# RMSNorm with doubled rows on one core: loads moved between the two DMA queues, the last tile loaded whole, and 60 drains at the head of two engines' programs

## Chip, cores and metric

The kernel runs on one core of a Trainium2 chip. The time is device time in microseconds (us). The kernel before took 240.69 to 241.01 us in four runs.

## The reference

```python
B, S, D = 8, 512, 2048
x_rep  = np.repeat(x, 2, axis=1)                       # every row twice
rms    = np.sqrt((x_rep ** 2).mean(axis=-1, keepdims=True) + 1e-6)
return ((x_rep / rms) * gamma[None, None, :]).astype(np.float32)
```

The input has 33.6 MB, the output 67.1 MB, all float32. Arithmetic is light (VectorE is busy 38% of the span and ScalarE 48%, the DMA engines 98.3%), so the work is mostly moving bytes.

## The kernel before

There are eight tiles of 128 partitions x 4 rows. A tile's buffer holds 8 rows: the input lands in rows 4 to 7, the results go to rows 0 to 7, and there are three buffers. ScalarE squares and sums a row and takes the root. VectorE inverts it and scales the row. The second copy of each row is made by ScalarE (three of four) or VectorE. Loads are issued on ScalarE's DMA queue, stores on SyncE's. The load of tile i+1 waits until the store of tile i-2 has left its buffer.

```python
    def load(i, eng, parts=1):
        y = rows.tile([P, K * R, D], f32, name="y")
        step = K // parts
        for k in range(0, K, step):
            at = K * (R - 1) + k
            eng.dma_start(out=y[:, at : at + step, :], in_=x_t[i, :, k : k + step, :])
        ys.append(y)

    def store(i, k0, k1):
        run = 32768 if i == ntiles - 3 else 65536
        nc.sync.dma_start(
            out=out_t[i, :, R * k0 * D : R * k1 * D],
            in_=ys[i][:, R * k0 : R * k1, :].rearrange("p j d -> p (j d)"),
            max_dma_last_dim=run,
        )
    # ... (square, scale, repeat, compute left out)
    load(0, nc.scalar, parts=K)
    gamma_b = singles.tile([P, D], f32, name="gamma_b")
    nc.sync.dma_start(out=gamma_b[0:1, :], in_=gamma.partition_broadcast(1))
    # ... (gamma's broadcast and eps left out)
    load(1, nc.scalar)
    load(2, nc.scalar)
    for i in range(ntiles):
        if i >= 2 and i + 1 < ntiles:
            load(i + 1, nc.scalar, parts=2 if i + 2 == ntiles else 1)
        parts = 2 if i == ntiles - 1 else 1
        for k in range(0, K, K // parts):
            compute(i, k, k + K // parts)
            store(i, k, k + K // parts)
```

Of the kernel before, what the change touches and what calls it, by code (L numbers as in the profile page):

```python
# [1 line left out]

# [4 lines left out]


@with_exitstack
def kernel(  # L10
    ctx: ExitStack,
    tc: tile.TileContext,
    x: bass.AP,
    gamma: bass.AP,
    out: bass.AP,
):
    nc = tc.nc
    P = nc.NUM_PARTITIONS
    f32 = mybir.dt.float32
    Act = mybir.ActivationFunctionType  # L20
    Alu = mybir.AluOpType

    B, S, D = x.shape
    Bo, So, Do = out.shape
    R = So // S
    assert R == 2 and D == Do and B == Bo and So == S * R
    eps = 1e-6
    inv_d = 1.0 / float(D)


    K = 4
    N = B * S
    assert N % (P * K) == 0
    ntiles = N // (P * K)
    x_t = x.rearrange("b s d -> (b s) d").rearrange("(n p k) d -> n p k d", p=P, k=K)
    out_t = out.rearrange("b s d -> (b s) d").rearrange("(n p j) d -> n p (j d)", p=P, j=K * R)

    singles = ctx.enter_context(tc.tile_pool(name="singles", bufs=1))
    rows = ctx.enter_context(tc.tile_pool(name="rows", bufs=3))
    junk = ctx.enter_context(tc.tile_pool(name="junk", bufs=1, space=bass.MemoryType.PSUM))  # L40
    small = ctx.enter_context(tc.tile_pool(name="small", bufs=8))

    ys = []
# [9 lines that stand above are left out]
        ys.append(y)  # L53

    def store(i, k0, k1):

        run = 32768 if i == ntiles - 3 else 65536
        nc.sync.dma_start(  # L58
            out=out_t[i, :, R * k0 * D : R * k1 * D],
            in_=ys[i][:, R * k0 : R * k1, :].rearrange("p j d -> p (j d)"),  # L60
            max_dma_last_dim=run,
        )

    def square(i, k):
        sq = junk.tile([P, D], f32, name="sq")
        ss = small.tile([P, 1], f32, name="ss")
        nc.scalar.activation(  # L67
            out=sq[:], in_=ys[i][:, K * (R - 1) + k, :], func=Act.Square, accum_out=ss[:]
        )
        rms = small.tile([P, 1], f32, name="rms")  # L70
        nc.scalar.activation(out=rms[:], in_=ss[:], func=Act.Sqrt, scale=inv_d, bias=eps_t[:])  # L71
        return rms

    def scale(i, k, rms):
        rstd = small.tile([P, 1], f32, name="rstd")
        nc.vector.reciprocal(out=rstd[:], in_=rms[:])  # L76
        nc.vector.scalar_tensor_tensor(  # L77
            out=ys[i][:, R * k, :], in0=ys[i][:, K * (R - 1) + k, :], scalar=rstd[:], in1=gamma_b[:],
            op0=Alu.mult, op1=Alu.mult,
        )  # L80

    def repeat(i, k, copy):
        copy(out=ys[i][:, R * k + 1, :], in_=ys[i][:, R * k, :])  # L83

    def compute(i, k0, k1):

        rms = square(i, k0)
        for k in range(k0, k1):
            scale(i, k, rms)
            if k + 1 < k1:  # L90
                rms = square(i, k + 1)
                repeat(i, k, nc.scalar.copy)
            else:
                repeat(i, k, nc.vector.tensor_copy)


    ctx.enter_context(tc.manual_schedule())
    load(0, nc.scalar, parts=K)
    gamma_b = singles.tile([P, D], f32, name="gamma_b")
    nc.sync.dma_start(out=gamma_b[0:1, :], in_=gamma.partition_broadcast(1))  # L100
    nc.gpsimd.partition_broadcast(out_ap=gamma_b[:], in_ap=gamma_b[0:1, :])  # L101
    eps_t = singles.tile([P, 1], f32, name="eps_t")
    nc.vector.memset(eps_t, eps)  # L103
    load(1, nc.scalar)
    load(2, nc.scalar)

    for i in range(ntiles):


        if i >= 2 and i + 1 < ntiles:  # L110
            load(i + 1, nc.scalar, parts=2 if i + 2 == ntiles else 1)
        parts = 2 if i == ntiles - 1 else 1
        for k in range(0, K, K // parts):
            compute(i, k, k + K // parts)
            store(i, k, k + K // parts)


# [1 line left out]
_INS = ['x', 'gamma']  # L119
_OUTS = [((8, 1024, 2048), 'float32')]  # L120


# [23 lines left out]
```

## Time and profile before

| | before |
|---|---|
| time, median of 3 runs | 240.72 us |
| span of the profiled run | 239.0 us |
| 16 DMA engines, two data queues | 98.3% of the span |
| ScalarE / VectorE busy | 48% / 38% |
| two 8 KB instruction packets at | 87.0 and 148.8 us |

The page of the kernel before, its first three parts. In part 2 a digit is the busy share of a fortieth of the span in tenths. In part 3 a line is a DMA queue (q1 is SyncE's, q10 ScalarE's, q14 the one that the page calls instruction) with packets, megabytes and its share of the 16 engines' time.

```profile
span 239.0 us, 295 instructions
...
DVE 90.8 (38%) x74; ACT 115.8 (48%) x121; POOL 2.5 (1%) x5
...
DMA  7999989989979989999899899799999999898994
...
q1 hardware_dynamic: 1426, 67.12, 65.0%
q10 hardware_dynamic: 1728, 33.56, 33.3%
q14 instruction: 2, 0.02, 0.0%
```

The DMA row stands at 7 to 9 tenths or more from the second slice to the last but one, and no compute engine comes near it. The kernel is bound by its DMA engines. The chain of waits agrees (part 4 of the page):

```profile
DMA 71%; ACT 10%; DVE 8%; ACTq 1%; issue 0%; SPq 0%
```

Such a row is an average over 16 engines. At the end each engine writes a packet of 4 bytes behind its last data packet, the first at 235.73 us and the last at 237.72 us. These are three stretches of the end, before. The last two columns are the mean busy share of the 16 DMA engines and GB/s.

```profile
core 0: us, DVE busy (x) ACT busy (x) POOL busy (x), PEclk, DMA share, GB/s
...
234.00:236.00 2.00, 0.00 (x0) 0.00 (x0) 0.00 (x0) 1.00 0.76 328
236.00:238.00 2.00, 0.00 (x0) 0.00 (x0) 0.00 (x0) 1.00 0.04 16
238.00:239.80 1.80, 0.00 (x0) 0.00 (x0) 0.00 (x0) 1.00 0.00 0
```

A share counts a packet where it starts, so a row can be over 1 (1.22 from 25 to 30 us) or a little early. One engine for the whole of a stretch is 1/16 = 0.06. After 236 us under one engine's worth starts, and after 238 us nothing.

The trace also has the single packets: start, duration, size and queue, but not the engine. 99.9% of the packets start within 5 ns of another packet's end, so each packet can be joined to the one that starts where it ends, and 16 sequences come out. The joining can swap two engines where packets end together. The 16 end times at the right don't depend on it. For the kernel before it gives, in us:

```
ends of the 16 engines, before: 235.74 235.81 235.94 235.98 236.02 236.04 236.08 236.13
                                236.15 236.16 236.18 236.24 236.50 236.70 236.71 237.72
usual duration: 64 KB 2.418 us, 32 KB 1.213, 16 KB 0.611, 8 KB 0.309
```

### The profile page before, as it was taken

Reading aid. Unit: us, or ns where it says so; the run is one execution under the profiler, and the core shown is the slowest. Engines: PE = TensorE matmul, PEld = TensorE weight load, DVE = VectorE, ACT = ScalarE, POOL = GpSimd, SP = SyncE. Lnnn points to the kernel's source line nnn. Section 1 sums busy time; section 2 is a strip of 40 time slices with the busy share of each in tenths; the row PEclk is TensorE's granted clock in tenths of the full one; section 3 lists DMA queues with packets and bytes.
Section 4 is the critical chain, followed back from the end, with each engine's and each line's share of the span. In section 5 each row is a group of like instructions: output and inputs, shape, how many; then the busy total and the mean of one; then the engine's idle time right before and its main releaser. Section 6 shows DMA issues by size and latency. Waiting matters only on the chain.

```text
span 239.0 us, 295 instructions
## 1 busy us (share of the span) xinstructions
DVE 90.8 (38%) x74; ACT 115.8 (48%) x121; POOL 2.5 (1%) x5
## 2 busy tenths in 40 slices
DVE  0477846006560047600666007460076490072000
ACT  3998992009940089500994019930499550180000
POOL 4000000000000000000000000000000000000000
DMA  7999989989979989999899899799999999898994
GB/s 267 428 447 439 439 351 439 526 351 439 515 345 455 450 374 494 395 411 510 362 428 526 351 439 528 345 444 433 400 430 444 406 499 436 384 505 356 439 428 192
DMA packets 3156, 100.69 MB, mean 421 GB/s; under 512 B 337, under 2 KB 337, under 8 KB 337
## 3 DMA queue, kind: packets, MB, share of 16 engines
q1 hardware_dynamic: 1426, 67.12, 65.0%
q10 hardware_dynamic: 1728, 33.56, 33.3%
q14 instruction: 2, 0.02, 0.0%
HBM read 33.56 MB, written 67.11 MB: 421 GB/s over the span
## 4 chain that ended last, share of the span: by engine, by line
DMA 71%; ACT 10%; DVE 8%; ACTq 1%; issue 0%; SPq 0%
DMA y<-in_x_dram 38%; DMA out_dram<-y 33%; DVE y L77 6%; ACT sq L67 6%; ACT y L83 3%; DVE y L83 2%; ACTq L52 1%; ACT rms L71 1%; DVE rstd L76 0%; SPq L58 0%
## 5 line engine op out<-in xcount | busy, mean ns | idle before, releaser
L67 ACT ACTIVATE sq<-y 128x2048 f32<-128x2048 f32 x32 | 59.9, 1872 | 90.3 <-DMA y<-in_x_dram 74.4
L77 DVE SCALAR_TENSOR_TENSOR y<-y,rstd,gamma_b 128x2048 f32<-128x2048 f32 x32 | 75.3, 2352 | 1.2
L76 DVE RECIPROCAL rstd<-rms 128x1 f32<-128x1 f32 x32 | 5.2, 162 | 123.6 <-ACT rms L71 123.6
L83 ACT COPY y<-y 128x2048 f32<-128x2048 f32 x23 | 43.4, 1888 | 3.6 <-DVE y L77 3.6
L83 DVE COPY y<-y 128x2048 f32<-128x2048 f32 x9 | 11.0, 1226 | 0.3
L71 ACT ACTIVATE rms<-ss,eps_t 128x1 f32<-128x1 f32 x32 | 9.4, 294 | 1.0
L67 ACT ACTIVATION_READ_ACCUMULATOR sq<-y 128x1 f32 x32 | 6.0, 186 | 0.0
L67 ACT ACT_TABLE_LOAD x1 | 1.3, 1283 | 4.1 <-issue 4.1
L101 POOL PARTITION_BROADCAST gamma_b<-gamma_b x1 | 2.3, 2295 | 2.4 <-DMA gamma_b<-in_gamma_dram 2.4
L71 ACT ACT_TABLE_LOAD x1 | 1.3, 1283 | 0.0
L103 DVE MEMSET eps_t<- 128x1 f32 x1 | 0.1, 59 | 0.8 <-PEq L130 0.8
L130 POOL MEMSET const-float32-0.0<- 128x1 f32 x1 | 0.1, 100 | 0.2 <-issue 0.2
L130 POOL MEMSET const-bfloat16-1.0<- 128x1 bf16 x1 | 0.1, 102 | 0.0
L130 POOL MEMSET const-uint8-127<- 128x1 uint8 x1 | 0.1, 102 | 0.0
L130 POOL MEMSET const-float32-1.0<- 128x1 f32 x1 | 0.1, 100 | 0.0
## 6 DMA issues: line engine op xcount, KB each, us to landing
y<-in_x_dram ACTq DMA_DIRECT2D x6, 4096.0 KB, 32.6
out_dram<-y SPq DMA_DIRECT2D x1, 8192.0 KB
out_dram<-y SPq DMA_DIRECT2D x2, 4096.0 KB, 26.4
y<-in_x_dram ACTq DMA_DIRECT2D x4, 1024.0 KB, 7.7
y<-in_x_dram ACTq DMA_DIRECT2D x2, 2048.0 KB, 29.9
out_dram<-y SPq DMA_DIRECT2D x6, 37.5
gamma_b<-in_gamma_dram SPq DMA_DIRECT2D x1, 8.0 KB
```

The lines of the kernel that those rows point to most:

```text
L52: eng.dma_start(out=y[:, at : at + step, :], in_=x_t[i, :, k : k + step, :])
L67: nc.scalar.activation(out=sq[:], in_=ys[i][:, K * (R - 1) + k, :], func=Act.Square, accum_out=ss[:])
L71: nc.scalar.activation(out=rms[:], in_=ss[:], func=Act.Sqrt, scale=inv_d, bias=eps_t[:])
L76: nc.vector.reciprocal(out=rstd[:], in_=rms[:])
L77: nc.vector.scalar_tensor_tensor(out=ys[i][:, R * k, :], in0=ys[i][:, K * (R - 1) + k, :], scalar=rstd[:], in1=gamma_b[:], op0=Alu.mult, o ...
L83: copy(out=ys[i][:, R * k + 1, :], in_=ys[i][:, R * k, :])
L101: nc.gpsimd.partition_broadcast(out_ap=gamma_b[:], in_ap=gamma_b[0:1, :])
L103: nc.vector.memset(eps_t, eps)
L130: nc = _bacc.Bacc("TRN2", target_bir_lowering=False, num_devices=1)
```

## The change

Its intent: start the first loads from the queue that is idle at the start and later serves the stores, and leave ScalarE's queue to the later loads. Load the last tile in one piece, drop the 32 KB store packets of one tile, and put instructions that do nothing at the head of ScalarE's and VectorE's programs, so that the two instruction packets of 87.0 and 148.8 us come at the start rather than in the middle.

```diff
     def store(i, k0, k1):
-        run = 32768 if i == ntiles - 3 else 65536
         nc.sync.dma_start(
             ...
-            max_dma_last_dim=run,
         )
 ...
-    load(0, nc.scalar, parts=K)
+    load(0, nc.sync, parts=K)
-    nc.sync.dma_start(out=gamma_b[0:1, :], in_=gamma.partition_broadcast(1))
+    nc.scalar.dma_start(out=gamma_b[0:1, :], in_=gamma.partition_broadcast(1))
 ...
-    load(1, nc.scalar)
-    load(2, nc.scalar)
+    for _ in range(60):
+        nc.scalar.drain()
+        nc.vector.drain()
+    load(1, nc.sync)
+    load(2, nc.sync)
     for i in range(ntiles):
         if i >= 2 and i + 1 < ntiles:
-            load(i + 1, nc.scalar, parts=2 if i + 2 == ntiles else 1)
+            load(i + 1, nc.scalar)
+        compute(i, 0, K)
         parts = 2 if i == ntiles - 1 else 1
         for k in range(0, K, K // parts):
-            compute(i, k, k + K // parts)
             store(i, k, k + K // parts)
```

## The prediction

> **What bounds the kernel now.** The 16 DMA engines. The page's DMA queues take 98.3% of their time (65.0% stores, 33.3% loads) over 239.0 us; VectorE is busy 38%, ScalarE 48%, and 71% of the chain of waits is DMA. By the single packet records all 16 engines work without a hole from about 2.6 to 235.3 us; an engine idles 3.5 us in all. A 64 KB packet takes 2.418 us (27.1 GB/s an engine): 100.7 MB need 232 us.
>
> Some 1 to 2 us are lost inside: (a) At 25.5 to 29.3 us, [...]load packets of 32 KB take up to 2.43 us instead of 1.213: about 1.2 us lost on each engine. (b) The engines' last packets end between 235.7 and 237.72 us, the last one 1.0 us behind the next. It had one of the two 8 KB instruction packets (148.8 us, 0.31 us long) and slow 32 KB store packets at 187 to 195 us, where four engines lost 0.4 to 1.0 us.
>
> **What the change does.**
> 1. Packets: 512 store packets of 32 KB (1.213 us) become 256 of 64 KB, and 256 load packets of 16 KB (0.611) become 128 of 32 KB: 2.0 + 1.2 us over 16 engines, 0.2 us saved.
> 2. Instruction pages: both fetches fell near the 64th instruction of ScalarE and of VectorE (87.0, 148.8 us). With the drains they come at the drains' end[...]. [...]this trace shows 8 KB packets. 0 to 0.6 us saved, on the last engine only.
> 3. First loads on the stores' queue: store 0 queues behind loads 1 and 2. Loss (a) may vanish or stay: 0 to 1.2 us.
> 4. Drains: [...] Store 0 is needed by 32 us and was issued at 23.8: off the critical path.
> 5. Tail: the last load's 32 KB packets alternate with 64 KB stores. I expect 33 us from issue (median before 32.6) instead of 39.7, so about 200 us; its first half is ready 11 us later (211), the second at 217.5. At 434 GB/s the last 8.4 MB take 19.4 us, so the halves are needed by 216 and 226 us. Slack of 5 and 8 us: no dry queue.
>
> **Critical:** only what the DMA engines save: 0.2 (packets), about 0.6 (evener end), about 0.4 (share of loss a). 240.7 - 1.2 = 239.5 us, range 238.4 to 240.9. Faster by over 2%: 0.01; within 2%: 0.97; slower: 0.02.
>
> **What would show it.** Data queues at 98 to 99% of the span; no idle slice before 235 us; instruction packets at 2 to 10 us, none in the middle; last engines within 1 us of each other; no long load packets at 27 us if step 3 pays; last load landing near 200 us, last store issued near 217 us.
>
> **What would make it wrong.** A dry queue at 205 to 216 us, if the last load lands 5 us later than I think; the four slow engines being chance of that run, not of the 32 KB packets; the step from loads to stores costing its 1.2 us in one queue too.

In the trace before, 29 load packets that start at 25.31 to 27.25 us are slow; store 0 was issued at 23.77 us, and its first 64 KB packet starts at 28.89 us.

## More of the kernel before

A run counts as slow when it is over 1.5% above the fastest of the same kernel in the same call.

In the trace, the second half of the last load has 16 landings from 204.67 to 208.04 us, and ScalarE's square that waits for it starts at 208.06 us, behind the last of them.

## The result, and the profile after

The changed kernel took 242.89 us (median of 4, 242.44 to 243.22) against 240.86 us for the kernel before (median of 4). The ratio is 1.0083, 95% interval 1.0065 to 1.0102. A ratio here is the mean time of one kernel's fast runs over that of the other's in the same rounds, so it is not quite the ratio of the medians quoted. It is 2 us slower, where a gain of 1.2 us was predicted (239.5 us, range 238.4 to 240.9).

The page after, the same lines as before:

```profile
span 241.1 us, 411 instructions
...
DVE 89.7 (37%) x73; ACT 117.4 (49%) x122; POOL 2.5 (1%) x5
...
DMA  6999999999998998999998998998998999899990
...
q1 hardware_dynamic: 2160, 79.69, 77.1%
q10 hardware_dynamic: 722, 20.98, 20.3%
q14 instruction: 3, 0.02, 0.0%
...
DMA 69%; ACT 13%; DVE 8%; SPq 1%; issue 0%
```

The DMA row has no hole, and the engines' share of the two data queues is 97.4% instead of 98.3%. Inside, both rows vary between 7 and 9; the change that stands out is the last slice, from 4 to 0. There lies the loss. The three stretches of the end, after:

```profile
234.00:236.00 2.00, 0.00 (x0) 0.00 (x0) 0.00 (x0) 1.00 0.61 262
236.00:238.00 2.00, 0.00 (x0) 0.00 (x0) 0.00 (x0) 1.00 0.15 66
238.00:239.80 1.80, 0.00 (x0) 0.00 (x0) 0.00 (x0) 1.00 0.08 36
```

Most engines stop earlier than before (0.61 against 0.76 in the first row), and the work of about two engines, then of one, goes on to the end (0.15 and 0.08, where one engine is 0.06). By the packets:

```
ends of the 16 engines, after: 235.44 235.54 235.55 235.55 235.61 235.67 235.70 235.74
                               235.87 235.88 235.89 235.90 235.92 235.98 239.67 239.71
```

Fourteen engines end by 235.98 us, and two go on for 3.7 us more. The last packet ends at 239.71 us against 237.72 before, which is 1.99 us later: the difference of the two times, within 0.1 us. The 14 themselves end about 0.4 us earlier (median 235.72; the other 15 of before 236.13).

What set two engines apart? The DMA queues in a window from 6.5 to 8 us of the changed kernel:

```profile
q1 hardware_dynamic: 87, 0.60, 99.1%
q14 instruction: 2, 0.02, 2.6%
```

Both instruction packets are here. In the kernel before, one such packet stood in each of these windows, 86.5 to 88 us and 148 to 149.5 us (the line is the same in both):

```profile
q14 instruction: 1, 0.01, 1.3%
```

In the single packets of the changed kernel the fetches run at 7.00 and 7.09 us for 0.309 us each, and the 8 KB load packet that follows each of them takes 0.86 us and 0.85 us instead of 0.309. Two engines are then about 0.86 us behind. They had lost 0.42 and 0.66 us in the kernel before (0.309, and 0.114 or 0.354 on the 64 KB packet that follows), much later. Later slow packets in the trace after stand almost all on late engines, in groups:

```
start us: time over the usual duration, ns, 50 or more (S = 64 KB store, L = 32 KB load)
 74.0 S 71    77.7 S 194, S 222    78.2 L 226    81.5 L 272, L 234
107.2 S 50, S 101    110.8 L 413, L 225
136.5 S 109          140.3 L 400, L 485    169.7 L 228, L 612    192.4 S 113    195.3 S 80    199.0 L 832
```

All the time over the usual durations after 33 us is about 5 us, or 2.5 us an engine if the two late ones bore it all. At the first switch from loads to stores, at about 31 us, they lose 1.6 us each where the median engine loses 1.0. With the 0.86 us that makes the 3.7 to 4 us.

**Theory 1**, from this reading: the drains move the instruction fetches to 7 us, each puts a DMA engine 0.86 us behind, and an engine that is behind loses more at each change between loads and stores. **Theory 2**: the first loads in the stores' queue make the late engines. **Theory 3**: the whole last load and the larger packets do.

### The profile page after: what moved, and what is told of

Its sections match the earlier page's. It is cut to its first block, busy times and chain, and to the rows that moved or that the text cites. A ratio compares the mean times of both kernels' runs of the same rounds, so it can differ in the third digit from the quotient of the medians.

```text
span 241.1 us, 411 instructions
## 1 busy us (share of the span) xinstructions
DVE 89.7 (37%) x73; ACT 117.4 (49%) x122; POOL 2.5 (1%) x5
## 4 chain that ended last, share of the span: by engine, by line
DMA 69%; ACT 13%; DVE 8%; SPq 1%; issue 0%
DMA y<-in_x_dram 36%; DMA out_dram<-y 33%; ACT sq L64 7%; DVE y L74 6%; ACT y L80 5%; DVE y L80 2%; ACT rms L68 1%; SPq L52 1%; DVE rstd L73 0%; SPq L56 0%
## 5 line engine op out<-in xcount | busy, mean ns | idle before, releaser
L80 ACT COPY y<-y 128x2048 f32<-128x2048 f32 x24 | 45.3, 1887 | 3.2 <-DVE y L74 3.2
L80 DVE COPY y<-y 128x2048 f32<-128x2048 f32 x8 | 9.8, 1226 | 0.3
```

Source lines behind the costliest of these rows:

```text
L80: copy(out=ys[i][:, R * k + 1, :], in_=ys[i][:, R * k, :])
```

## The experiments

All kernels below gave correct results. "Before" is the kernel before, run between them on the same chip. Every edit is against the kernel that is named.

### First call: the drains, the queues

It ran on a chip that was disturbed in part: the kernel before took 240.5 to 240.8 us four times, and 248.22, 246.44 and 245.76 us three times. Each kernel's first run has the profile.

**a_nodrain**: the changed kernel without drains.

```diff
-    for _ in range(60):
-        nc.scalar.drain()
-        nc.vector.drain()
```

> The changed kernel without its 120 drains. Theory 1 (early instruction fetch): in the changed kernel the two 8 KB instruction packets at 7.0 us put two DMA engines about 0.9 us behind the other 14, and an engine out of step loses more at each change between loads and stores, so that the two end 3.7 us late. Then without drains the fetches fall at about 85 and 145 us again, no engine ends over 1.7 us behind the rest, and the time is 239.8 to 240.9 us. Theory 2 (first loads in the stores' queue): the lag comes from the queues, so this stays at 242 to 243 us with two engines over 3 us late. Theory 3 (whole last load and 64 KB packets): the same 242 to 243 us as theory 2.

Measured: 248.09, 248.47, 245.46 and 244.84 us. All three theories missed. In its profile the slow packets stand on most engines from 110 us on, and the queues ran dry for a time: 313 GB/s between 212 and 230 us, where VectorE and ScalarE were still computing the last tile. I took this for a disturbed run and did not count it.

**b_drain**: the kernel before with the drains.

```diff
+    for _ in range(60):
+        nc.scalar.drain()
+        nc.vector.drain()
     load(1, nc.scalar)
```

> The kernel before with the 60 drains on ScalarE and VectorE added before load 1, all else as it was. Theory 1: two engines fall behind at about 7 us and end 3 to 4 us late: 242.3 to 243.5 us. Theories 2 and 3: drains are free here, 240.5 to 241.2 us.

Measured: 242.96 us in the profiled run, then 246.27 to 246.49 us in disturbed rounds. So one undisturbed run is all that it has. The profile of the 242.96 us run is clear: fetches at 7.3 and 9.2 us, one engine ending at 239.87 us, three at 237.1 to 237.3, the other 12 by 236.13. That agrees with theory 1, with one engine over 3 us late where I expected two.

**b_queues**: the kernel before with the queues of the changed one for loads 0 to 2 and gamma.

```diff
-    load(0, nc.scalar, parts=K)
+    load(0, nc.sync, parts=K)
 ...
-    nc.sync.dma_start(out=gamma_b[0:1, :], in_=gamma.partition_broadcast(1))
+    nc.scalar.dma_start(out=gamma_b[0:1, :], in_=gamma.partition_broadcast(1))
 ...
-    load(1, nc.scalar)
-    load(2, nc.scalar)
+    load(1, nc.sync)
+    load(2, nc.sync)
```

> The kernel before with only the queues changed (loads 0 to 2 on SyncE's queue, gamma on ScalarE's), no drains, last tile and packet sizes as before. Theory 1: 240.2 to 241.2 us, no engine over 1.7 us late. Theory 2: 242 to 243 us. Theory 3: as before, 240.5 to 241.2 us.

Measured: 244.06 us in the profiled run, 246.53 to 246.99 us after it. The profile has an engine that ends at 240.98 us with no early fetch (87.0 and 152.4 us). Its first slow load packets after 33 us stand at 109.5, 130.3 and 139.1 us (0.30, 0.32 and 0.84 us over). That spoke for theory 2 and against theory 1. It also shows that an engine can become late without an early lag, in disturbed rounds at least.

**a_dve**: the changed kernel with drains on VectorE alone.

```diff
     for _ in range(60):
-        nc.scalar.drain()
         nc.vector.drain()
```

> The changed kernel with the drains on VectorE only. Theory 1: one early fetch at about 7 us instead of two, ScalarE's fetch back at about 85 us: one engine ends over 3 us late instead of two, the time stays at 242 to 243.2 us since the last engine sets it. If the lag needs both fetches, or ScalarE's, 240 to 241 us. Theories 2 and 3: 242 to 243 us with two late engines.

Measured: 242.81 us in the profiled run, 243.79 to 246.1 us after it. The profile has one fetch at 6.9 us and one at 89.4 us. One engine ends at 239.68 us, the other 15 between 235.38 and 236.04 us. The end of it, in the same stretches:

```profile
236.00:238.00 2.00, 0.00 (x0) 0.00 (x0) 0.00 (x0) 1.00 0.08 33
238.00:239.80 1.80, 0.00 (x0) 0.00 (x0) 0.00 (x0) 1.00 0.04 18
```

The shares are half of those of the changed kernel (0.15 and 0.08): one late engine instead of two, and the same end. One early fetch makes one late engine. There is no third fetch here, so the one at 192.1 us in the changed kernel is not needed for the lag.

### Second call: the same without disturbance, and the tail

It ran on the same chip. The before runs are pooled with those of the first call; the one new one took 240.24 us.

**a_nodrain2**, the same as a_nodrain:

> The same as a_nodrain, since that call was disturbed (the kernel before took up to 248 us in it). Theory 1 (an early instruction fetch puts an engine out of step, and it loses more at each change between loads and stores): 239.8 to 241.2 us in undisturbed runs, last engine at most 1.7 us behind the bulk. Theory 2 (first loads in the stores' queue) and theory 3 (whole last load): 242 to 243 us. If it is slower than the changed kernel here too (244 us or more), theory 1 falls and the drains help.

Measured: one fast run of 239.45 us, three slow ones of 249.48, 245.87 and 245.95 us. One kernel shows both 239.45 and 249.48 us, so the 245 to 248 us of the first call are slow. A single fast run is little, and it was repeated again (a_nodrain3).

**b_queues2**, the same as b_queues:

> The same as b_queues, whose profile had an engine 4.7 us late with no early fetch, in the disturbed call. Theory 1: 240.2 to 241.5 us, last engine at most 1.7 us late. Theory 2: 242 to 244 us again with an engine 3 us late or more, which would show the queue change alone enough to make a late engine.

Measured: 239.87 and 240.65 us fast, 248.64 and 245.31 us slow. In the profile of the 239.87 us run the fetches are at 86.9 and 148.6 us and the 16 engines end between 235.6 and 236.8 us. The late engine of the first call is gone with the same program, so theory 2 falls: moving the first loads costs nothing that these two fast runs show, and a_nodrain3 below, which has the move too, agrees.

**a_drain30**: the changed kernel with 30 drains.

```diff
-    for _ in range(60):
+    for _ in range(30):
```

> The changed kernel with 30 drains instead of 60, so that the fetches fall at about 35 us (ScalarE) and 57 us (VectorE). Theory 1: the lag has fewer tiles to grow in, the last engine 1.5 to 3 us late, 240.8 to 242.4 us, between no drains and 60. Theories 2 and 3: 242 to 243 us.

Measured: 243.9 to 246.68 us, outside what any theory expected. The fetches fell at 20.6 and 61.6 us, not at 35 and 57 us as I had expected. In the profile all engines are late: twelve end at 238.2 to 238.6 us, four at 240.4 to 241.0. The engines were idle for 0.9 us each between 210 and 220 us. This may be the slow state, as none of its runs was undisturbed by the look of it. It is inconclusive.

**b_tail**: the kernel before with the tail of the changed one.

```diff
-        run = 32768 if i == ntiles - 3 else 65536
 ...
-            max_dma_last_dim=run,
 ...
-            load(i + 1, nc.scalar, parts=2 if i + 2 == ntiles else 1)
+            load(i + 1, nc.scalar)
+        compute(i, 0, K)
 ...
-            compute(i, k, k + K // parts)
```

> The kernel before with only the tail changed: last load whole, its tile computed whole and stored in halves, no 32 KB store packets. Theory 3: 242 to 243 us, the queue running dry before the last stores or engines ending unevenly. Theories 1 and 2: within 0.5 us of before, 240.2 to 241.2 us.

Measured: 241.17, 240.91 and 240.99 us, and a slow one of 245.63. The ratio to before is 1.0015 (0.9993 to 1.0038). Fifteen engines end by 236.05 us, one at 238.03. Theory 3 falls: by the ratio the tail costs 0.4 us, and at most 0.9 us by the interval, where 2 us were to be explained. It brought no gain that shows.

### Third call: a lag without a fetch

It ran on another chip. Before: nine fast runs of 239.69 to 242.66 us, two slow ones.

**a_nodrain3**, the same as a_nodrain:

> The changed kernel without drains a third time, for undisturbed runs (one run of 239.45 us so far). Theory 1: fast runs 239.2 to 240.2 us, about 1% under the changed kernel and 0.3 to 0.6% under the kernel before.

Measured: 240.78, 240.47, 240.83, 239.89 and 242.09 us fast, one slow of 245.8. The ratio to before is 0.9998 (0.9949 to 1.0046). Without drains the loss of 2 us is gone: the interval lies wholly under those of the changed kernel (1.0065 to 1.0102, and 1.0052 to 1.0123 later on this same chip). The gain that I expected on top is not there, so the other parts of the change together are worth nothing that these runs can show. The end of its profiled run:

```profile
234.00:236.00 2.00, 0.00 (x0) 0.00 (x0) 0.00 (x0) 1.00 0.65 279
236.00:238.00 2.00, 0.00 (x0) 0.00 (x0) 0.00 (x0) 1.00 0.04 16
238.00:239.80 1.80, 0.00 (x0) 0.00 (x0) 0.00 (x0) 1.00 0.00 0
```

Fifteen engines end by 236.07 us and one, with the fetch of 148.7 us, at 237.64: the same picture as before the change. Taking out the 32 KB store packets did not by itself even the end.

**a_lag_early**: no drains, and one engine is given 0.93 us more work early (three rows of gamma, 3 x 0.309 us, into rows of a tile that are free until 54 us).

```diff
     load(2, nc.sync)
+    for r in range(3):
+        nc.scalar.dma_start(out=ys[2][0:1, r, :], in_=gamma.partition_broadcast(1))
```

> No drains; three extra 8 KB rows are loaded on ScalarE's queue at about 2 to 6 us into a spare row of tile 2, each one packet, all on one DMA engine: 0.93 us more work for it and no instruction fetch. It tells what the early fetch did: if a lag of that size grows by itself (theory 1 with growth), that engine ends 3 us or more behind the bulk and the time is 242 to 243.5 us, as with drains. If a lag does not grow (the fetch does something else), the engine ends about 1 to 1.5 us behind and the time is 239.8 to 240.8 us.

Measured: 242.19 to 243.12 us in six runs, ratio 1.0071 (1.0039 to 1.0104). Fourteen engines end by 236.05 us, one (with the later fetch) at 236.75, and one at 239.61.

```profile
234.00:236.00 2.00, 0.00 (x0) 0.00 (x0) 0.00 (x0) 1.00 0.69 295
236.00:238.00 2.00, 0.00 (x0) 0.00 (x0) 0.00 (x0) 1.00 0.04 16
238.00:239.80 1.80, 0.00 (x0) 0.00 (x0) 0.00 (x0) 1.00 0.04 18
```

The three packets ran at 4.96, 5.88 and 6.80 us. This settles the first half. An early lag of 0.9 us on one engine ends as 3.8 us behind the median of the 14 (235.85 us), with no drain and no early fetch in the program. Of this, 2.1 us are four load packets at 81.6, 140.1, 169.5 and 199.0 us. The fetch is only the cause of the lag; what it costs comes from the growth.

**a_lag_late**: the same three rows beside the load of tile 6, issued at 139 us.

```diff
             load(i + 1, nc.scalar)
+            if i == 5:
+                for r in range(3):
+                    nc.scalar.dma_start(out=ys[6][0:1, r, :], in_=gamma.partition_broadcast(1))
```

> No drains; the same three extra rows, but loaded at about 138 us, beside the load of tile 6. With growth: fewer changes between loads and stores are left, so the engine ends 1.3 to 2.7 us behind, 240.3 to 242 us, clearly under the early one. Without growth: the same as the early one, 239.8 to 240.8 us.

Measured: 241.69 to 242.84 us, ratio 1.0059. The experiment was badly made. The three small packets stood in the loads' queue behind load 6, with store packets between them, and ran only at 173.0, 178.1 and 184.1 us, and the scaling of tile 6 had to wait for them. Store 6 was issued at 197.9 us instead of 188.8 us (a_nodrain3), and the engines were idle for 1.5 us each around 195 us. It measures that wait, not the lag.

**a_act**: drains on ScalarE alone.

```diff
     for _ in range(60):
         nc.scalar.drain()
-        nc.vector.drain()
```

> The changed kernel with the drains on ScalarE only. Theory 1: ScalarE's fetch at about 7 us, VectorE's back at about 145 us; one engine over 3 us late, 242 to 243.2 us. If the lag is VectorE's fetch alone: 239.5 to 240.5 us.

Measured: 243.25 to 248.29 us. In the profiled run (246.48 us) slow packets stand on most engines from 60 us on, and all engines end between 241.0 and 243.3 us. It looks slow, and it is inconclusive.

### Fourth call: one queue for everything

By then I thought that a late engine falls into the opposite order of load and store packets, because its packets come from two queues. That was my guess. What the packets show is the order itself: on 13 of the 16 sequences of the changed kernel a 32 KB load and a 64 KB store alternate five times in a tile, and then two loads and later two stores stand together; the other three, the two late ones among them, have a different order in some tiles. If two queues are the cause, there should be no such growth with one.

**one_queue**: no drains, and the later loads on SyncE's queue too.

```diff
-            load(i + 1, nc.scalar)
+            load(i + 1, nc.sync)
```

> No drains, and every load and store on SyncE's queue (gamma alone stays on ScalarE's)[...]. If the growth of a lag comes from engines that fall into the opposite order of load and store packets, it can't happen here: 239.0 to 240.3 us in nearly every run, no runs at 244 us or more, last engine at most 1.7 us behind. If the order is not the cause, runs as for a_nodrain3 (239.9 to 242, and some at 245 or more).

Measured: 241.0 to 242.32 us in six runs, none slow, ratio 1.002 (0.9989 to 1.0051). It is later than I expected. No run went to 244 us or above, though the kernel before did so three times.

**one_queue_lag**: the same, with the three early rows of a_lag_early.

> The same with the three extra 8 KB rows on one engine at 2 to 6 us. If opposite order is the cause of growth: the lag stays what it is, that engine ends 0.9 to 1.6 us behind, 239.8 to 241.2 us, well under the 242.6 us of a_lag_early. If a lag grows for another reason: 242 to 243.5 us again.

Measured: 242.05 to 242.69 us, ratio 1.006. One engine ends at 239.56 us, the others by 236.70.

**one_queue_drain**: the changed kernel with the later loads on SyncE's queue.

> The same with the 60 drains instead, the fetches at about 7 us. If opposite order is the cause: the two engines end about 0.9 to 1.6 us behind, 239.8 to 241.2 us. If the early fetch costs the time by itself: 242 to 243.5 us.

Measured: 243.02 to 243.32 us, ratio 1.0091 (1.005 to 1.0132). Two engines end at 239.55 and 239.80 us, the others by 236.90. Against the median of one_queue itself (241.43 us) one_queue_lag is 1.1 us later and this 1.7 us.

So the lag grows as much with a single queue, and the theory of opposite order falls. The packets of one_queue_lag show what is left of it, since here loads and stores come in blocks. The late engine and another one:

```
late:   ... 77.82 L  79.03 L  80.24 L +988 ns   82.44 L  83.65 S  86.07 S ...
other:  ... 77.71 L  78.92 L  80.13 L +63 ns    81.41 S  83.82 S  86.24 S ...
```

The others begin to store at about 81.4 us. The late engine is still loading, and the load packet that runs while they begin takes 2.20 us instead of 1.213. At the next block, near 109 us, it is 0.25 and 0.11 us more, near 197 us 0.49.

I counted the same over the profiled runs of after, a_dve, a_lag_early, a_lag_mid (below), a_nodrain3, one_queue_lag and one_queue_drain, from 33 to 200 us. For each 32 KB load packet, take the share of the other engines' packet time beside it that went to stores:

```
others storing    packets   mean over 1.213 us   more than 0.2 us over
under 20%           3224          1.6 ns                6
20 to 40%           1112          6.3 ns               14
40 to 80%             89        113.6 ns               18
80% and over          53         32.4 ns                3
```

A load in step with the others is hardly ever slow (6 of 3224). A load that meets the others in the middle of their switch is slow by more than 0.2 us in one case of five (18 of 89), and this is where many of a late engine's loads stand. This is a count of loads alone, not an experiment: it shows where the time is lost, not why.

**after2**, the changed kernel beside them:

> The changed kernel itself once more, beside the three and on the same chip: 242.3 to 243.3 us, or more in the second state; two engines (or more) 3 us or more behind the bulk.

Measured: 242.88 to 243.36 us, ratio 1.0087: the result stands. The expected picture does not. In the profiled run three engines ended at 238.8, 239.4 and 240.2 us and the rest at 238.0 to 238.1, so that the last was 2.1 us behind the rest and not 3. The last load landed at 206.7 us instead of 203.9, and the engines were idle for 1.4 us each between 210 and 220 us: the dry queue that the prediction had named as a risk. So the same time is not always made up in the same way.

### Fifth call: does the lag grow with the switches that are left?

It ran on a third chip. Before: ten fast runs, 239.82 to 241.07 us.

**a_lag_mid**: the three rows again, on the stores' queue behind store 4, where nothing waits for them.

```diff
             load(i + 1, nc.scalar)
+            if i == 5:
+                for r in range(3):
+                    nc.sync.dma_start(out=ys[6][0:1, r, :], in_=gamma.partition_broadcast(1))
```

> No drains; the three extra 8 KB rows on one engine again, but late, on the stores' queue behind store 4, so that they run at about 165 to 170 us and nothing waits long for them. If a lag grows at each switch from loads to stores (a load packet that is still running when the others begin to store takes 0.2 to 1.2 us more), only the switches at about 170 and 199 us are left: 1.5 to 2.6 us behind at the end, 240.3 to 241.6 us, between a_nodrain3 (240.5) and a_lag_early (242.6). If a lag of this size jumps to 3.6 us whenever it comes: 242 to 243 us.

Measured: 240.79, 240.79, 242.18, 240.66 and 240.78 us fast, 245.99 slow; ratio 1.002 (0.9995 to 1.0046). The rows ran at 168.2 to 169.3 us. One engine ends at 237.83 us, one (with the fetch of 152 us) at 237.04, the other 14 by 236.21.

```profile
236.00:238.00 2.00, 0.00 (x0) 0.00 (x0) 0.00 (x0) 1.00 0.04 16
238.00:239.80 1.80, 0.00 (x0) 0.00 (x0) 0.00 (x0) 1.00 0.00 0
```

The same work on one engine, 160 us later, makes 2.0 us of lag behind the median of the 14 instead of 3.8, and hardly any time on the clock, as some engine was that late anyhow. The size is as expected, but the place is not. The late engine loses nothing on loads at the switches of 170 and 199 us. It loses 0.21 us on one of the rows and 0.80 us on store packets at 176.6 to 187.8 and 195.1 us.

**a_lag_end**: three rows of 7 KB after the last computation.

```diff
+    extra = singles.tile([1, 1792], f32, name="extra")
+    for r in range(3):
+        nc.scalar.dma_start(out=extra[:, :], in_=gamma.partition_broadcast(1)[:, 0:1792])
```

> No drains; three extra rows of 7 KB on one engine after the last computation, from about 217 us, when no load is left and all engines only store. Growth at switches: none left, so that engine ends about 0.8 to 1.2 us behind the bulk, beside the engine that had the fetch at 148 us (1.6 to 1.8 us behind), and the time stays at 239.9 to 241 us. If a lag grows with time or by packets: more than 1.5 us, 241.5 us or more.

Measured: fast runs of 239.64, 240.93, 241.0, 242.27, 241.09 and 241.21 us, two slow; ratio 1.0018 (0.9986 to 1.0051). The times lie near the upper end of what no growth expects. The profiled run was a slow one (248.19 us), so its time says nothing. But the engine can be followed in it. The rows ran at 229.8, 236.2 and 242.5 us among stores alone, and their engine ends at 244.01 us, 1.0 us behind the median of 14 others (243.03). That is what was put in: 0.82 us for the rows and 0.25 us for one slow packet beside the first. So this lag did not grow, over the 14 us that were left to it. It speaks for the theory and does not prove it.

The slow profiles show one thing more. In a_lag_end and a_nodrain2, one and three of the 16 joined sequences lose 6.7 to 8.1 us each in slow packets after 33 us, with no early fetch and no early row in the program, and the engines then stand idle for about 6 us each between 160 and 230 us. So some engines fall far behind and the others run dry. What starts it there is not shown.

## Why the prediction was wrong

- **What bounds the kernel**: right. The DMA engines are full to 235 us in both profiles, and after the change the first 14 engines end within 0.6 us of each other (before, within 1.0 us).
- **Packets, 0.2 us saved**: right in direction. The bulk of the engines ends about 0.4 us earlier, which is more than the packets alone can give. It did not reach the clock, as the last engine sets it.
- **Drains off the critical path**: right for the engines that execute them. ScalarE's first table load starts at 3.75 us after, 4.09 before, and store 0 is issued at 23.84 us against 23.77. An instruction packet does not hold up ScalarE visibly either: in the kernel before, its square beside the one of 87.0 us takes 1.86 us, and all 32 squares take 1.86 to 1.88.
- **Instruction pages: this is the step that failed.** The prediction said "0 to 0.6 us saved, on the last engine only", and "about 0.6 (evener end)". The fetches did move to the start, to 7.0 and 7.1 us (predicted 2 to 10). But there each cost its DMA engine 0.86 us, against 0.42 and 0.66 us in the kernel before, and by the end two engines were 3.7 us behind the last of the others. The term was not +0.6 us of gain but 2.0 us of loss: the last packet ends at 239.71 instead of 237.72 us. I treated an engine's lag as a sum that comes out the same wherever it starts. a_lag_early and a_lag_mid show that it is not: 0.93 us of extra work is 3.8 us at the end if it comes at 5 to 7 us, and 2.0 us if it comes at 168 us. In both runs the rows fell on the engine that also carries gamma's row, by the bytes of its sequence, so the lag was tried on that engine alone. Nor does every lag grow: the 0.42 us of the fetch at 87.0 us in the kernel before left no engine visibly late. The other half of the evener end, no 32 KB store packets, brought nothing by itself either: b_tail and a_nodrain3, without drains, still end with one engine at 238.03 and 237.64 us, against 237.72 before.
- **"None in the middle"** was wrong too: a third instruction packet came at 192.1 us. (Every instruction packet from 1 us on has 8,192 bytes, in both traces.) It is not needed for the loss (a_dve has none).
- **Loss (a), the step from loads to stores, 0.4 us expected**: too high. Between 20 and 35 us an engine loses 1.09 us on average after the change and 1.24 before, so at most 0.15 us came of it. With the loads in one queue with the stores, load packets at 30 to 32 us still take 0.6 to 1.3 us longer than usual (up to 2.54 us; before, up to 2.43), and store 0, issued at 23.84 us, sends its first packet at 32.33 us, behind the loads. The prediction had named this as what would make it wrong.
- **Tail**: the last load landed at 203.9 us, not 200, because it was issued 2 us later (170.1) and took 33.8 us. Without drains (a_nodrain3) it was issued at 168.0 and landed at 201.8 us. The last store was issued at 220.9 us, not 217. The queue did not run dry in that profile. The chain of waits has the piece; start, duration and what it is, before and then after:

```profile
168.39 39.65 DMA y<-in_x_dram
```

```profile
170.08 33.80 DMA y<-in_x_dram
```

What is shown: the drains cause the loss (a_nodrain3 without them 0.9998; a_dve, where one early fetch gives one late engine), and an early lag of one engine grows without any early fetch (a_lag_early). What is supported but not shown: that the growth happens at the switches between loads and stores. The slow loads of a_lag_early and one_queue_lag speak for it, and so does the lag of a_lag_end, which did not grow among stores alone. The slow stores of a_lag_mid, away from the two switches, speak against it as the only place. What is open: why a packet takes longer on an engine that is out of step with the others, and what starts the slow state of 244 to 249 us.

No version clearly beat the kernel before. The fastest single run came from a variant without drains (239.45 us), but the kernel before has runs of 239.69 and 239.70 us, and with more runs a_nodrain3 was level with it.

## What to carry to other kernels

In this kernel, where the data queues took 97.4 to 98.3% of the 16 DMA engines' time, the slowest engine set the time (after the change 14 ended by 235.98 us and the last at 239.71 us), so look at the end of a trace engine by engine and not at their mean. A small piece of work that falls on a single DMA engine, such as a one-row load or an instruction fetch, need not be free, and in this kernel it cost more when it came early: 0.9 us in the first 7 us became 3.8 us, and at 168 us it became 2.0 us. Do not pull an instruction fetch forward into a saturated stretch to "get it over with" before you have checked which is the last engine.
